# One joining pass for both head groups on eight tiles, T64's last block by VectorE's transposes, and kq products moved ahead, in a two-layer gated DeltaNet and attention encoder

## The chip, the cores and the metric

The kernel runs on one core of a Trainium2 chip. The metric is the device time of one execution in microseconds (us). Before the change it is 744.85, the median of three runs (744.83 to 745.56).

## The reference, cut to what matters

Two layers, 256 tokens of 1024 channels, float32. Each layer normalises its input, multiplies it with one wide input weight, runs two mixers on the parts (a: gated DeltaNet, b: differential attention, 8 heads each), projects both (w_pa, w_pb), merges them with two sigmoid gates and projects again (w_out). The change lies in the DeltaNet mixer. Per head and direction it needs, for each chunk of tokens, the inverse T of a unit lower triangular matrix:

```python
L = jnp.where(strict, jnp.einsum('bhncd,bhnmd->bhncm', kb, k) * decay, 0.0)
T = lax.linalg.triangular_solve(eye + L, jnp.broadcast_to(eye, L.shape),
                                left_side=True, lower=True, unit_diagonal=True)
u = jnp.einsum('bhncm,bhnme->bhnce', T, vb)
w = jnp.einsum('bhncm,bhnmd->bhncd', T, kb * jnp.exp(g)[..., None])
qk = jnp.where(lower, jnp.einsum('bhncd,bhnmd->bhncm', q, k) * decay, 0.0)
```

It runs once forwards and once backwards over the tokens; the two results are added, normalised and gated with silu(z). The attention mixer takes two softmaxes per head, their weighted difference times v, a normalisation per head and a gate with silu(z).

## The kernel before

**Work and order.** TensorE does the projections as chains of 128x512 matmuls in split float32 (a weight and an activation each as a high and a low part, three products: high by high, high by low, low by high; L324 to L326). A projection of 512 columns has 8 k-tiles of 6 matmuls. In the stretch that matters here the projections are, in this order, zb, za (gates of the mixers), gb, ga (the b and the a gate), pb; each has two halves of 512 columns (gb0, gb1, ...). Their 16 k-tiles each give the places 0 to 79: `place(32)` is the first k-tile of gb0, 39 the last, 47 the last of gb1, 48 the first of ga0. All else on TensorE is hung behind such a place (`behind(ins)`), and a scheduler fixes one order for each engine when the kernel is built; every engine works its own queue strictly in that order.

**Weights.** A quarter of a projection's weights (two k-tiles) is loaded by SyncE's queue (`raw_`), cast to the high part by ScalarE (`hi_`, L308) and subtracted to the low part by VectorE (`lo_`, L310). For gb1's second quarter both parts live in `wgb`.

**The triangular inverse.** The kernel treats a chunk of 128 tokens per head, both directions. A forward substitution makes the inverses of the 32-wide diagonal blocks; they go through DRAM into `U_` (transposed blocks, one tile for both groups of four heads) and `T64` (plain blocks, one tile for each group; L898 to L911). Then blocks are joined to 64, then to 128.
- 64-wide joining, in `merges(g)`, once for each group g: y64 = A-block times T64-block, 32 products of 32x32 (L924), copied by ScalarE (L928); zt = y64 transposed times U-block, 32 products (L938), negated by ScalarE into U's off-diagonal blocks (L950); z, the plain form of half of them, 16 products (L943), negated by ScalarE into T64 (L953). Each product works on the 32x32 tile of TensorE's array given by its operands' partitions (rows) and its result's (columns). With `srcdst` these are four tiles, one to a strip of 32 rows, the same four for both groups; z uses two.
- 128-wide joining, in `join()` for both groups at once: y128 = A-block times T64 (64x64, four tiles), copied (L971, L973), then zt with U, negated into U (L981).
- `chunks(g)` then uses U for the recurrence (y1p, sp, ks, y2p, qs, po; L995, L1034).

The steps of `merges` and `join` are placed by a list (L1265): both groups' y64 behind the first kq block (pseudo place 41), zt and z of group 0 at 43, of group 1 at 45, y128 at 48, its zt at 50.

**kq and q's sums.** `weigh_q(g, c)` multiplies k by q for four heads (`gram`, L787, 4 products, called the kq block (g, c) here) and VectorE weighs the result into B (L828). The four of a layer are placed at 39, 42, 44 and 47. `key_sums` (L1042) squares q: VectorE transposes (`tb_q`, L135), ScalarE squares, VectorE sums, then a trip through DRAM on GpSimd's queue and a last sum `ssq` (L1056).

**The attention's end.** The last head's attention (`turn(7)`, `attend(7)`: at and av, L1097 and L1108) stands in gb0 and gb1. ScalarE copies av to `ob` and squares it twice (`sqj`, L1112, L1114), the sums `ssb` go through VectorE (L1239, L1240), GpSimd's power and VectorE (`rb`, L1242); `gate_yb` then gates ob (L1200), transposes it in blocks (`zb`, L249) and sends it through DRAM on GpSimd's queue (L251, L257) to become `ybT` (L263, L265), the input of pb.

PSUM tiles named `bank` and `bank_c` have two buffers each: a third tile waits until the first has been read.

Of the kernel before, what the change touches and what calls it, by code (L numbers as in the profile page):

```python
# [8 lines left out]
F32 = mybir.dt.float32  # L9
# [8 lines left out]
P = 128  # L18
# [3 lines left out]
NM = SEQ // P  # L22
# [27 lines left out]
def hybrid_encoder(  # L50
# [53 lines left out]
    mark = {}  # L104
# [402 lines left out]
    for l in range(DEPTH):  # L507
# [389 lines left out]
        def merges(g):  # L897
# [15 lines left out]
            v4 = lambda ap: ap.rearrange("p (c h i) -> p c h i", c=NM, h=4)  # L913
            y64p = v4(bank_c(f"y64p{l}{g}")[:, :256])
            y64 = work.tile([P, NM, 4, 32], F32, tag="w2c", name=f"y64{l}{g}", bufs=3)

            order = [(c, j4, mm, d) for c, j4 in every for mm in range(2) for d in range(2)]
            order.sort(key=lambda k: k != (0, 0, 1, 1))
            first = mark["pin"]
            for n_, (c, j4, mm, d) in enumerate(order):  # L920
                b0, b1 = srcdst(d, mm)
                co = 32 * (b0 % 2)
                with behind(first):
                    mm_ = T.matmul(y64p[blk(b1), c, j4, :], A[blk(b0), g, c, j4, blk(b1)],  # L924
                                   T64[blk(b0), tix(d, c, j4), co : co + 32], start=True, stop=True)
                if n_ == 0:
                    first = mm_.ins
            S.copy(y64, y64p)  # L928
            yield
            first = mark["pin"]  # L930
            zt64 = v4(bank_c(f"zt64{l}{g}")[:, :256])
            z64 = v4(bank_c(f"z64{l}{g}")[:, :256])
            for c, j4 in every:
                for mm in range(2):
                    for d in range(2):
                        b0, b1 = srcdst(d, mm)
                        with behind(first):
                            T.matmul(zt64[blk(b0), c, j4, :], y64[blk(b1), c, j4, :],  # L938
                                     U[blk(b1), tix(d, c, j4), blk(b1)], start=True, stop=True)
            for c, j4 in every:  # L940
                for d in range(2):
                    b0, b1 = srcdst(d, d)
                    T.matmul(z64[blk(b1), c, j4, :], U[blk(b1), tix(d, c, j4), blk(b1)],  # L943
                             y64[blk(b1), c, j4, :], start=True, stop=True)
            for d in range(2):
                td = slice(8 * d, 8 * d + 8)
                fl = lambda z, b: z[blk(b)].rearrange("p c h i -> p (c h) i")
                for mm in range(2):
                    b0, b1 = srcdst(d, mm)
                    S.mul(U[blk(b0), td, blk(b1)], fl(zt64, b0), -1.0)  # L950
                b0, b1 = srcdst(d, d)
                co = 32 * (b0 % 2)
# [277 lines left out]
        wgb = big.tile([P, 2, 2, 512], F32R, tag="p8", name=f"wgb{l}", bufs=4)  # L1230
        gtb = gate(C_GB, f"gb{l}", "ev",
# [162 lines left out]
```

## Time and profile before

| | before |
|---|---|
| median of three runs | 744.85 us |
| the profiled execution | 744.91 us |
| its span in the profile | 743.0 us |
| TensorE busy | 734.2 us (99%) |
| VectorE busy | 584.4 us (79%) |
| ScalarE busy | 482.2 us (65%) |
| GpSimd busy | 141.0 us (19%) |
| chain that ended last, TensorE's share | 96% |

The span is the time between the first and the last instruction that the profiler saw; the execution's own time holds 1.9 us more around it. A timeline row gives start, length, engine, line, operation, output and inputs by the program's names, shape and number of records merged; in brackets the idle time ahead of it and what ended it. TensorE overlaps matmuls, so the time from one start to the next tells what a matmul costs, not its length. Both layers have the same stretch; in the first it lies from about 219 us to 300 us.

### The profile page before, as it was taken

To read this page: it belongs to the slowest core of one execution; us is meant where nothing else is said; L and a number is where in the kernel's file an instruction comes from. 1 tells how busy PE (TensorE), PEld (TensorE's weight loads), DVE (VectorE), ACT (ScalarE), POOL (GpSimd) and SP (SyncE) were. 2 spreads that over 40 slices of the span, in tenths; PEclk is the share of its full clock that TensorE was granted. 3 is DMA by queue.
4 is the path that set the end of the run, shared out by engine and by line. 5 is a ranking of instruction groups with operands and counts; after the bars stand their busy time and mean duration, and the time that the engine had idled before them with its cause. 6 is when DMAs were issued, how large, how long until landed. Compare 5 with 4: busy or idle time off the path is not lost.

```text
span 743.0 us, 13901 instructions
## 1 busy us (share of the span) xinstructions
PE 734.2 (99%) x5162; PEld 637.3 (86%) x5162; DVE 584.4 (79%) x1111; ACT 482.2 (65%) x1024; POOL 141.0 (19%) x223
## 2 busy tenths in 40 slices
PE   9999999999999999999999999999999999999996
PEld 6999889987888889888889899889788888998885
DVE  8696898999986865578667769899999669538782
ACT  6667875667877586645456578565687758665552
POOL 5004110112022442100000150202110425301000
PEclk9999999999999999999999999999999999999999
DMA  8765667776666462557675466768666747335641
GB/s 262 238 173 170 173 182 198 206 212 196 209 182 175 152 186 89 173 203 244 202 233 141 124 194 192 213 174 230 197 173 197 199 129 224 108 121 204 215 141 57
DMA packets 73733, 135.45 MB, mean 182 GB/s; under 512 B 12912, under 2 KB 13921, under 8 KB 73666
## 3 DMA queue, kind: packets, MB, share of 16 engines
q1 hardware_dynamic: 64750, 113.65, 51.3%
q0 software_dynamic: 7936, 19.35, 8.9%
q10 hardware_dynamic: 980, 1.58, 0.6%
q8 instruction: 40, 0.66, 0.4%
q14 instruction: 27, 0.22, 0.1%
HBM read 125.53 MB, written 9.01 MB: 181 GB/s over the span
## 4 chain that ended last, share of the span: by engine, by line
PE 96%; ACT 2%; issue 1%; DVE 1%; POOLq 0%; POOL 0%; DVEq 0%; ACTq 0%
PE pp_vb L369 4%; PE pp_qk L325 4%; PE pp_qk L326 3%; PE pp_qk L324 3%; PE sc L1070 2%; PE pp_o L369 2%; PE pp_za L325 2%; PE pf_k L385 2%; PE pf_v L385 2%; PE pf_v L389 2%; PE pp_gb L325 2%; PE pp_gb L324 2%; PE pp_zb L324 2%; PE pf_q L387 2%; PE pf_k L389 2%; PE pf_k L387 2%
## 5 line engine op out<-in xcount | busy, mean ns | idle before, releaser
L325 PE MATMUL pp_qk<-lo_qk,hT 128*128 128x512 f32 x128 | 50.5, 394 | 0.3
L326 PE MATMUL pp_qk<-hi_qk,hT 128*128 128x512 f32 x128 | 49.9, 390 | 0.0
L310 DVE TENSOR_TENSOR lo_qk<-raw_qk,hi_qk 128x1024 fp32r<-128x1024 f32 x32 | 39.1, 1221 | 11.1 <-ACT hi_qk L308 10.8
L324 PE MATMUL pp_qk<-hi_qk,hT 128*128 128x512 f32 x128 | 45.1, 393 | 0.0
L308 ACT CAST hi_qk<-raw_qk 128x1024 fp32r<-128x1024 f32 x28 | 29.4, 1050 | 23.4 <-PE pp_qk L326 12.4
L1080 ACT ACTIVATE es<-sc,mx 128x256 f32<-128x256 f32 x64 | 29.7, 474 | 19.6 <-DVE mx L1078 19.6
L310 DVE TENSOR_TENSOR lo_pb<-raw_pb,hi_pb 128x1024 fp32r<-128x1024 f32 x16 | 19.6, 1225 | 24.5 <-ACT hi_pb L308 24.5
L385 PE MATMUL pf_q<-hT,hi_q 128*128 128x256 f32 x128 | 36.1, 285 | 0.0
L387 PE MATMUL pf_q<-hT,hi_q 128*128 128x256 f32 x128 | 35.9, 284 | 0.0
L385 PE MATMUL pf_k<-hT,hi_k 128*128 128x256 f32 x128 | 35.9, 286 | 0.0
L387 PE MATMUL pf_k<-hT,hi_k 128*128 128x256 f32 x128 | 35.9, 285 | 0.0
L385 PE MATMUL pf_v<-hT,hi_v 128*128 128x256 f32 x128 | 35.8, 285 | 0.0
L387 PE MATMUL pf_v<-hT,hi_v 128*128 128x256 f32 x128 | 35.8, 284 | 0.0
L389 PE MATMUL pf_q<-hT,lo_q 128*128 128x256 f32 x128 | 35.2, 288 | 0.0
L389 PE MATMUL pf_v<-hT,lo_v 128*128 128x256 f32 x128 | 34.6, 288 | 0.0
L389 PE MATMUL pf_k<-hT,lo_k 128*128 128x256 f32 x128 | 34.3, 283 | 0.0
L308 ACT CAST hi_pa<-raw_pa 128x1024 fp32r<-128x1024 f32 x16 | 16.9, 1055 | 22.2 <-PE pp_pa L326 16.1
L679 DVE SCALAR_TENSOR_TENSOR cvq<-pf_q,cw,cvq 128x254 f32<-128x254 f32 (+1 forms) x64 | 29.9, 478 | 0.9 <-ACT cvq L675 0.4
L679 DVE SCALAR_TENSOR_TENSOR cvv<-pf_v,cw,cvv 128x254 f32<-128x254 f32 (+1 forms) x64 | 29.8, 476 | 0.1
L325 PEld LDWEIGHTS pp_qk<-lo_qk,hT 128*128 128x128 f32 x128 | 24.0, 188 | 6.7 <-DVE lo_qk L310 1.7
L679 DVE SCALAR_TENSOR_TENSOR cvk<-pf_k,cw,cvk 128x254 f32<-128x254 f32 (+1 forms) x64 | 28.4, 476 | 1.5 <-ACT cvk L675 0.9
L310 DVE TENSOR_TENSOR lo_pa<-raw_pa,hi_pa 128x1024 fp32r<-128x1024 f32 x16 | 19.6, 1224 | 11.2 <-ACT hi_pa L308 11.2
(417 smaller groups left out, 2536.9 us busy)
## 6 DMA issues: line engine op xcount, KB each, us to landing
raw_qk<-in_w_in_dram SPq DMA_DIRECT2D x32, 512.0 KB, 3.8
raw_k<-in_w_in_dram SPq DMA_DIRECT2D x16, 512.0 KB, 4.6
raw_q<-in_w_in_dram SPq DMA_DIRECT2D x16, 512.0 KB, 3.8
raw_v<-in_w_in_dram SPq DMA_DIRECT2D x16, 512.0 KB, 3.8
raw_zb<-in_w_in_dram SPq DMA_DIRECT2D x16, 512.0 KB, 3.9
raw_za<-in_w_in_dram SPq DMA_DIRECT2D x16, 512.0 KB, 3.8
raw_ga<-in_w_in_dram SPq DMA_DIRECT2D x16, 512.0 KB, 4.5
raw_pb<-in_w_pb_dram SPq DMA_DIRECT2D x16, 512.0 KB, 3.8
```

What stands on the lines that cost most here:

```text
L308: high = (V.tensor_copy if kp in turned else S.copy)(hi[:, :, :n], raw[:, :, :n]).ins
L310: mark[nm, kp] = high, V.tensor_tensor(lo[:, :, :n], raw[:, :, :n], hi[:, :, :n].bitcast(F32), ALU.subtract).ins
L324: T.matmul(o, act[kt // 4][:, 0, kt % 4, ts_], hi, start=kt == 0, stop=False)
L325: T.matmul(o, act[kt // 4][:, 0, kt % 4, ts_], lo, start=False, stop=False)
L326: mark["proj"] = T.matmul(o, act[kt // 4][:, 1, kt % 4, ts_], hi, start=False, stop=kt == KT - 1).ins
L369: mark["proj"] = T.matmul(o, act[kt // 4][:, pa, kt % 4, ts_], ws[kt][1 + pw], start=kt == 0 and n_ == 0, stop=kt == KT - 1 and n_ == 2).ins
L385: T.matmul(o, hi[:, cs], act[kt // 4][:, 0, kt % 4, :], start=first, stop=False, skip_group_check=True)
L387: T.matmul(o, hi[:, cs], act[kt // 4][:, 1, kt % 4, :], start=False, stop=False, skip_group_check=True)
L389: T.matmul(o, lo[:, cs], act[kt // 4][:, 0, kt % 4, :], start=False, stop=done, skip_group_check=True)
L679: V.scalar_tensor_tensor(ca[:, o0:o1], acc[:, b, o0 + sft : o1 + sft], cw[:, j, cb : cb + 1], ca[:, o0:o1], ALU.mult, ALU.add)
L1070: mm = T.matmul(sp[n][:, qt * SEQ : (qt + 1) * SEQ], qkT[h // 4][rows, 0, h % 4, qt * P : (qt + 1) * P], qkT[h // 4][rows, 1, h % 4, :], s ...
L1080: S.activation(es[:, n, qt, :], spv[:, qt, :], AF.Exp, bias=mx[:, n, qt : qt + 1], accum_out=s_all[:, h, n, qt : qt + 1])
```

## The change

The 64-wide joining moves from `merges` into `join` and is done for both groups in one pass. Group 1 writes its y64 and zt two blocks of 32 further on (`across`), so that the two groups work on eight tiles of the array, two in each strip of rows. The z products and their PSUM tiles are gone: ScalarE negates zt into U, four pieces first, and VectorE transposes these four in 32x32 blocks from U into T64; then ScalarE negates the other four. ScalarE copies group 1's y64 in two halves. The list of steps becomes y64 behind kq (1,0), zt at 44, y128 at 47 and its zt at 49.

The kq blocks and the last head move: kq (0,0) to place 32, at of head 7 at 34, kq (0,1) to 36, av of head 7 and kq (1,0) to 39, kq (1,1) to 42. q's transposes wait for the a gate's fourth quarter (`ga0`, 3) and not for the last weighing. The second part of `gate_yb` is placed one weight quarter later.

The core of the diff:

```diff
+        def join():
+            across = lambda b, g: (b + 2 * g) % 4
...
+            order = [(c, j4, s2, d, g) for c, j4 in every for g in range(2) for s2 in range(2) for d in range(2)]
...
+                    made = T.matmul(y64p[g][blk(across(b1, g)), c, j4, :], A[blk(b0), g, c, j4, blk(b1)],
+                                    parts[g][1][blk(b0), tix(d, c, j4), co : co + 32], start=True, stop=True)
...
-            S.copy(y64, y64p)
+            S.copy(y64[0], y64p[0])
+            for h_ in range(2):
+                S.copy(y64[1][halves[h_]], y64p[1][halves[1 - h_]])
...
-                    T.matmul(z64[blk(b1), c, j4, :], U[blk(b1), tix(d, c, j4), blk(b1)],
-                             y64[blk(b1), c, j4, :], start=True, stop=True)
...
-                S.mul(T64[blk(b1), td, co : co + 32], fl(z64, b1), -1.0)
...
+                                T.matmul(zt64[g][blk(across(b0, g)), c, j4, :], y64[g][blk(b1), c, j4, :],
+                                         parts[g][0][blk(b1), tix(d, c, j4), blk(b1)], start=True, stop=True)
+            for own in (True, False):
+                for g in range(2):
...
+                        S.mul(U[blk(b0), td, blk(b1)], fl(zt64[g], across(b0, g)), -1.0)
+                        if own:
+                            co = 32 * (b0 % 2)
+                            V.transpose(T64[blk(b1), td, co : co + 32], U[blk(b0), td, blk(b1)])
...
-                with behind(mark["weighed"]):
+                with behind(mark[f"ga{l}0", 3][1]):
                     turn_squares(tb, kq[:, h : h + 2, :, 1, :].rearrange("p h m t -> p (h m) t"))
...
+        def last_head():
+            weigh_q(0, 0, place(32))
+            aT = turn(7, es[7], place(34))
+            weigh_q(0, 1, place(36))
+            attend(7, aT, place(39))
+            weigh_q(1, 0, place(39))
...
-                   (lambda: attend(7, turn(7, es[7], place(34)), place(39)),
-                    lambda: [weigh_q(n // 2, n % 2, place((39, 42, 44, 47)[n])) for n in range(4)]),
+                   (last_head, lambda: weigh_q(1, 1, place(42))),
...
-            at = [mark[f"ga{l}0", m][1] if i else mark[f"gb{l}1", 2 + m][1] for m in range(NM)]
+            at = [mark[f"ga{l}0", 1 + m][1] if i else mark[f"gb{l}1", 2 + m][1] for m in range(NM)]
...
-            mark["pin"] = mark["kq", 0, 0] if at == 41 else place(at)
+            mark["pin"] = mark["kq", 1, 0] if at == 41 else place(at)
...
-        order = [(mg[:2], 41), (mg[:1], 43), (mg[1:2], 45), (mg[2:], 48), (mg[2:], 50)]
+        order = [(mg[2:], 41), (mg[2:], 44), (mg[2:], 47), (mg[2:], 49)]
```

What the scheduler made of it is seen in each engine's row order. VectorE in layer 0, from the split of gb1's last weight quarter (`lo_gb`) to that of ga0's first (`lo_ga`), before; `B` is a weighing of kq, `ob` the gating of y_b, `zb` its transposes:

```order
L310 TENSOR_TENSOR lo_gb_2817<-raw_gb_2818,hi_gb_2816 128x1024
L828 TENSOR_TENSOR B_371<-kq_2834,B_371 128x1024
L1239 TENSOR_TENSOR ssb_382<-ssb_382,r_2860 128x16
L1240 TENSOR_TENSOR ssb_382<-ssb_382,r_2860 128x16
L828 TENSOR_TENSOR B_371<-kq_2840,B_371 128x1024
L1242 SCALAR_TENSOR_TENSOR rb_2862<-rb_2862,r_2860 128x16
L1200 SCALAR_TENSOR_TENSOR ob_0_383<-ob_0_383,rb_2862,zb_0_385 128x128 x8
L249 STREAM_TRANSPOSE zb_0_385<-ob_0_383 128x4x4x32 x2
L828 TENSOR_TENSOR B_371<-kq_2846,B_371 128x1024
L310 TENSOR_TENSOR lo_ga_2896<-raw_ga_2897,hi_ga_2895 128x1024
```

The same stretch after the change, where `T` is T64 (one tile for each group):

```order
L310 TENSOR_TENSOR lo_gb_2835<-raw_gb_2836,hi_gb_2834 128x1024
L1242 TENSOR_TENSOR ssb_382<-ssb_382,r_2860 128x16
L828 TENSOR_TENSOR B_371<-kq_2770,B_371 128x1024
L1243 TENSOR_TENSOR ssb_382<-ssb_382,r_2860 128x16
L828 TENSOR_TENSOR B_371<-kq_2852,B_371 128x1024
L1245 SCALAR_TENSOR_TENSOR rb_2862<-rb_2862,r_2860 128x16
L1197 SCALAR_TENSOR_TENSOR ob_0_383<-ob_0_383,rb_2862,zb_0_385 128x128 x8
L249 STREAM_TRANSPOSE zb_0_385<-ob_0_383 128x4x4x32 x2
L954 STREAM_TRANSPOSE T_2651<-U__96 32x8x32 x2
L954 STREAM_TRANSPOSE T_2658<-U__96 32x8x32 x2
L310 TENSOR_TENSOR lo_ga_2896<-raw_ga_2897,hi_ga_2895 128x1024
```

The third kq weighing (kq_2770, block (1,0)) now stands between the two steps of ssb, the fourth ahead of rb, and the T64 transposes stand behind the gating of y_b and its transposes.

ScalarE from the copy of head 7's av (`ob`) to the copies of y64, before; the cast of gb1's last quarter stands first:

```order
L308 CAST hi_gb_2816<-raw_gb_2818 128x1024
L1112 COPY ob_1_384<-av_2750 128x2x128
L1114 ACTIVATE sqj_312,ssb_382<-ob_1_384 128x128 x2
L928 COPY y_3230<-y64p_3229 128x256
L928 COPY y_3265<-y64p_3264 128x256
L950 ACTIVATE U__96<-zt_3299 32x8x32 x4
L953 ACTIVATE T_2651<-z_3300 32x8x32 x2
```

and after:

```order
L1109 COPY ob_1_384<-av_2762 128x2x128
L1111 ACTIVATE sqj_312,ssb_382<-ob_1_384 128x128
L308 CAST hi_gb_2834<-raw_gb_2836 128x1024
L1111 ACTIVATE sqj_312,ssb_382<-ob_1_384 128x128
L932 COPY y_3231<-y64p_3229 128x256
L934 COPY y_3232<-y64p_3230 64x256 x2
L951 ACTIVATE U__96<-zt_3300 32x8x32 x3
```

The cast now stands between the two squares of ob whose sums VectorE's ssb needs.

On TensorE the wide gb matmuls of a layer (48 of gb0, 48 of gb1) now have between them: av of head 6 with kq (0,0) after 26, at of head 7 after 38, kq (0,1) after 48, av of head 7 after 57, kq (1,0) and all of y64 after 65, kq (1,1) after 66, all of zt after 78, and y128 after 96. Before, av of head 7 with kq (0,0) and y64 stood after 62, and y128 behind ten matmuls of ga0. The 128-wide zt now stands after 21 of ga0, y1p after 36.

More of the change, by code (lines that the diff above doesn't have):

```diff
@@ L912, in merges @@
             yield
+        def join():
             v4 = lambda ap: ap.rearrange("p (c h i) -> p c h i", c=NM, h=4)
[L914 to L918, printed above, removed]
+            fl = lambda z, b: z[blk(b)].rearrange("p c h i -> p (c h) i")
+            across = lambda b, g: (b + 2 * g) % 4
+            y64p = [v4(bank_c(f"y64p{l}{g}")[:, :256]) for g in range(2)]
+            y64 = [work.tile([P, NM, 4, 32], F32, tag="w2c", name=f"y64{l}{g}", bufs=3) for g in range(2)]
+            order = [(c, j4, s2, d, g) for c, j4 in every for g in range(2) for s2 in range(2) for d in range(2)]
+            order.sort(key=lambda k: k[:4] != (0, 0, 1, 1))
@@ L919, in merges @@
             first = mark["pin"]
-            for n_, (c, j4, mm, d) in enumerate(order):
-                b0, b1 = srcdst(d, mm)
+            for n_, (c, j4, s2, d, g) in enumerate(order):
+                b0, b1 = srcdst(d, s2)
                 co = 32 * (b0 % 2)
                 with behind(first):
[L924 to L927, printed above, removed]
@@ L928, in merges @@
-            S.copy(y64, y64p)
+                    made = T.matmul(y64p[g][blk(across(b1, g)), c, j4, :], A[blk(b0), g, c, j4, blk(b1)],
+                                    parts[g][1][blk(b0), tix(d, c, j4), co : co + 32], start=True, stop=True)
+                if n_ < 2:
+                    first = made.ins
+            S.copy(y64[0], y64p[0])
+            for h_ in range(2):
+                S.copy(y64[1][halves[h_]], y64p[1][halves[1 - h_]])
             yield
-            first = mark["pin"]
@@ L931, in merges @@
-            zt64 = v4(bank_c(f"zt64{l}{g}")[:, :256])
-            z64 = v4(bank_c(f"z64{l}{g}")[:, :256])
+            zt64 = [v4(bank_c(f"zt64{l}{g}")[:, :256]) for g in range(2)]
             for c, j4 in every:
-                for mm in range(2):
-                    for d in range(2):
[L936 to L943, printed above, removed]
-                             y64[blk(b1), c, j4, :], start=True, stop=True)
[L945 to L952, printed above, removed]
-                S.mul(T64[blk(b1), td, co : co + 32], fl(z64, b1), -1.0)
+                for g in range(2):
+                    for s2 in range(2):
+                        for d in range(2):
+                            b0, b1 = srcdst(d, s2)
+                            with behind(mark["pin"]):
+                                T.matmul(zt64[g][blk(across(b0, g)), c, j4, :], y64[g][blk(b1), c, j4, :],
+                                         parts[g][0][blk(b1), tix(d, c, j4), blk(b1)], start=True, stop=True)
@@ new lines, in join @@
+            for own in (True, False):
+                for g in range(2):
+                    U, T64 = parts[g]
+                    for d in range(2):
+                        td = slice(8 * d, 8 * d + 8)
+                        b0, b1 = srcdst(d, d if own else 1 - d)
+                        S.mul(U[blk(b0), td, blk(b1)], fl(zt64[g], across(b0, g)), -1.0)
+                        if own:
+                            co = 32 * (b0 % 2)
+                            V.transpose(T64[blk(b1), td, co : co + 32], U[blk(b0), td, blk(b1)])
@@ L954, in merges @@
             yield
-        def join():
-            v4 = lambda ap: ap.rearrange("p (c h i) -> p c h i", c=NM, h=4)
             every4 = [(c, j4, g, d) for c, j4 in every for g in range(2) for d in range(2)]
```

## The prediction

> **What bounds the kernel now.** I read the page first, then who TensorE waited for, then the timeline of TensorE around the joining, and last those of ScalarE and VectorE at the same place.
>
> ```profile
> span 743.0 us, 13901 instructions
> PE 734.2 (99%) x5162; PEld 637.3 (86%) x5162; DVE 584.4 (79%) x1111; ACT 482.2 (65%) x1024; POOL 141.0 (19%) x223
> PE idle L410 <- DVE ones L407: 1.1, 1, 1.1
> PE pp_vb L464 <- ACT wktm_vb L308: 0.3, 1, 0.3
> PE pp_vb L464 <- ACT hT L234: 0.2, 1, 0.2
> PE pp_vb L464 <- DVE wktm_vb L310: 0.2, 1, 0.2
> ```
>
> The first two lines are the page's, the other four the whole answer on TensorE's waits (who waited, for whom, total, times, longest). TensorE is busy 99% of the span, and its four waits lie in the opening. So TensorE's stream sets the end: what it no longer does is gained in full, and any new wait of it is lost in full.
>
> The next rows are TensorE's timeline in layer 0 (start, length, line, tiles, shape, records; a float32 product leaves two records). First the y64 products of both groups with a kq block behind them:
>
> ```profile
> 237.11 0.38 PE L1108 MATMUL av<-vb,aT 128*128 128x128 f32 x2
> ...
> 238.98 1.47 PE L924 MATMUL y64p<-T,A 32*32 32x32 f32 x128
> 240.38 0.50 PE L325 MATMUL pp_gb<-wgb,hT 128*128 128x512 f32 x1
> 240.71 0.39 PE L326 MATMUL pp_gb<-wgb,hT 128*128 128x512 f32 x1
> ...
> 241.41 1.05 PE L787 MATMUL kq<-kq 128*128 128x128 f32 x8
> 242.22 0.47 PE L324 MATMUL pp_gb<-wgb,hT 128*128 128x512 f32 x1
> 242.53 0.39 PE L325 MATMUL pp_gb<-wgb,hT 128*128 128x512 f32 x1
> ...
> 602.16 1.47 PE L924 MATMUL y64p<-T,A 32*32 32x32 f32 x128
> ```
>
> Then the second group's zt and z products, the end of the b gate's projection and the y128 products:
>
> ```profile
> 250.07 0.39 PE L324 MATMUL pp_gb<-hi_gb,hT 128*128 128x512 f32 x1
> 250.39 0.75 PE L938 MATMUL zt<-U__96,y 32*32 32x32 f32 x64
> 251.00 0.69 PE L943 MATMUL z<-y,U__96 32*32 32x32 f32 x32
> 251.62 0.50 PE L325 MATMUL pp_gb<-lo_gb,hT 128*128 128x512 f32 x1
> 251.96 0.40 PE L326 MATMUL pp_gb<-hi_gb,hT 128*128 128x512 f32 x1
> ...
> 253.70 0.48 PE L324 MATMUL pp_ga<-hi_ga,hT 128*128 128x512 f32 x1
> 254.01 0.40 PE L325 MATMUL pp_ga<-lo_ga,hT 128*128 128x512 f32 x1
> ...
> 255.83 0.39 PE L324 MATMUL pp_ga<-hi_ga,hT 128*128 128x512 f32 x1
> 256.15 1.16 PE L964 MATMUL y128p<-T,A 64*64 64x64 f32 x64
> 257.24 0.50 PE L325 MATMUL pp_ga<-lo_ga,hT 128*128 128x512 f32 x1
> ```
>
> What to see: the wide matmuls stand (255.83 - 254.01)/8 = 0.228 us apart. A kq block of 8 records costs 242.53 - 241.41 - 0.23 = 0.89, so 0.11 a record and nothing for its edges. The y64 block holds 1.40 up to the next matmul. A zt and z block costs 251.96 - 250.07 - 2 x 0.228 = 1.43: 0.61 for 64 records of zt on four tiles (9.5 ns each), 0.62 for 32 of z on two tiles (19 ns each), 0.20 for edges. Half the tiles, twice the time a record: the tile is what is slow (38 ns a record), not the issue. The second layer has the same block 363.2 us later, so I work out layer 0 and double it.
>
> **What TensorE itself saves, per layer.** z goes, and the two zt blocks become one, on eight tiles. Now: 2 x 1.43 = 2.87. After: 128 records, 0.20 of edges and about 0.13 of drain (what y64 and z show above pace). If eight tiles halve the pace to 4.75 ns, that is 0.61 + 0.33 = 0.94, a saving of 1.93; if they stay at 9.5, it is 1.55, a saving of 1.32. y64 goes from 1.40 to 0.74, or stays. The four kq blocks, av and at remain as many and only move. So TensorE's own share lies between 1.32 and 2.59.
>
> Which end is likelier hangs on tiles that share a strip of 32 rows, as the eight do in pairs. y128 has four tiles of 64, two to a strip: 16 rounds in 1.09 us, 68 ns a round. Taking turns, 64 columns would cost 34 ns, less than the 38 of zt's 32. So they run at once, and I lean to 2.59. The Trainium skill, page "TensorE: Matmul & The Clock Gate", Part 3, "The mechanism", speaks against it: a weight load overlaps running matmuls only where the row group differs. By that rule the pairs would take turns, and the share would be 1.32; the y128 rows do not bear it out.
>
> **What waits instead.** y128 reads T64, whose last piece came from z by ScalarE. Now VectorE transposes it out of U, and VectorE has it in a fixed order behind the gating of y_b. I follow that queue. ScalarE:
>
> ```profile
> 237.18 1.05 ACT L308 CAST hi_gb<-raw_gb 128x1024 fp32r<-128x1024 f32 x1 [1.50 <-DMA raw_gb<-in_w_in_dram]
> 238.87 0.37 ACT L1112 COPY ob<-av 128x256 f32<-128x256 f32 x1 [0.64 <-PE av L1108]
> 239.27 0.31 ACT L1114 ACTIVATE sqj<-ob 128x128 f32<-128x128 f32 x1
> ...
> 239.71 0.31 ACT L1114 ACTIVATE sqj<-ob 128x128 f32<-128x128 f32 x1
> ...
> 245.27 1.54 ACT L950 ACTIVATE U__96<-zt 32x256 f32<-32x256 f32 x4 [4.17 <-PE zt L938]
> ```
>
> and VectorE, with a group of transposes of a like form last:
>
> ```profile
> 238.25 1.23 DVE L310 TENSOR_TENSOR lo_gb<-raw_gb,hi_gb 128x1024 fp32r<-128x1024 f32 x1 [1.81 <-ACT hi_gb L308]
> 239.40 1.22 DVE L828 TENSOR_TENSOR B<-kq,B 128x1024 f32<-128x1024 f32 x1
> 240.53 0.17 DVE L1239 TENSOR_TENSOR ssb<-ssb,r 128x16 f32<-128x16 f32 x1
> 240.73 0.18 DVE L1240 TENSOR_TENSOR ssb<-ssb,r 128x16 f32<-128x16 f32 x1
> ...
> 244.38 0.18 DVE L1242 SCALAR_TENSOR_TENSOR rb<-rb,r 128x16 f32<-128x16 f32 x1 [0.65 <-POOL rb L156]
> 244.59 2.19 DVE L1200 SCALAR_TENSOR_TENSOR ob<-ob,rb,zb 128x128 f32<-128x128 f32 x8
> 246.69 2.01 DVE L249 STREAM_TRANSPOSE zb<-ob 128x512 f32<-128x512 f32 x2
> 248.55 1.21 DVE L828 TENSOR_TENSOR B<-kq,B 128x1024 f32<-128x1024 f32 x1
> ...
> 278.62 0.26 DVE L1056 TENSOR_REDUCE ssq<-qss 128x16 f32<-128x64 f32 x1 [4.42 <-DMA qss<-qdr]
> ...
> 299.82 0.69 DVE L1036 TENSOR_TENSOR kq<-po,kq 128x512 f32<-128x512 f32 x1 [1.85 <-PE po L1034]
> ```
>
> ```profile
> L135 DVE STREAM_TRANSPOSE tb_q<-kq x8: 656/694/708, 259.0 to 629.8; 128x512 f32<-128x512 f32 x8
> ```
>
> The order of the changed program is: head 7's av, copy, first square, a cast of hi_gb, second square (ScalarE); split of lo_gb, ssb, weighing of kq (1,0), ssb, rb, gating, two transposes, then the four T64 transposes (VectorE). With the steps of these rows, in us of this trace:
> - av of head 7 comes five wide matmuls earlier and behind two kq blocks: 237.11 - 1.14 + 1.78 = 237.75. Its copy started 1.76 after the block's start, when kq's records took turns with av's; six records fewer (0.67) make it 1.09: 238.84.
> - First square +0.40: 239.24. The cast +0.44: 239.68. Its data landed at 237.18 and move by a kq block at most, so they don't hold it.
> - lo_gb starts 1.07 after the cast (238.25 - 237.18): 240.75; ssb +1.15: 241.90; weighing +0.20: 242.10; second ssb +1.13: 243.23. That is 2.50 later than before (240.73).
> - rb +3.65 (the power on GpSimd between): 246.88; gating +0.21: 247.09; transposes +2.10: 249.19; the first T64 transpose +1.86: 251.05.
> - A T64 transpose is 32 x 256 and not in this trace. At half of tb_q's length on top of a fixed part like ssb's: 0.17 + (0.69 - 0.17)/2 = 0.43, and 0.35 apart. Least: plain half, 0.35, 0.27 apart. Most: half of zb's slower pace (1.86/2 = 0.93 apart), 0.63 and 0.55 apart. I take the first, since tb_q too writes whole runs of 32. The fourth is done at 251.05 + 1.05 + 0.43 = 252.53 (least 252.21, most 253.33).
>
> y128's second group cannot start before that. Its first 16 records then have two tiles, the other 32 all four, so the block still needs 1.09: it ends at 252.53 + 0.05 + 1.09 = 253.67. Without the ten a gate matmuls that stood ahead (253.70 to 255.83 and one more, 2.36), it would have ended at 257.24 - 2.36 = 254.88 before. So a layer gains 1.21. TensorE alone would be through at 254.88 - 2.59 = 252.29 to 253.56; it waits 0.1 to 1.4 us, and the pace of eight tiles hardly matters.
>
> **The other edits, at nothing.** ScalarE copies y64 in three pieces and negates zt in eight at 0.385 (1.54/4): 3.1 us. It sat idle 4.17 before that, and 18 wide matmuls, 4.1 us, lie between zt and y128, which needs those banks; gone, that cover would cost what is over 4.1. The first low part of the a gate's weights queues behind the T64 transposes on VectorE, done at about 253.7; TensorE wants it one matmul after y128, at 254.0. If the transposes slip, both slip. q's sums move behind the a gate's fourth part with their store and loads on GpSimd's queue; ssq was there at 278.62, and its first reader follows the products added from 299.82, so some 15 us cover it. On GpSimd the four loads of one y_b tile now go ahead of the next tile's store, on SP one a-gate load goes behind the norm weights: both feed work of later projections. Weighing kq earlier fills VectorE's gaps (1.81 before lo_gb) and is in the steps above.
>
> **Sum.** 2 x 1.21 = 2.4 us. The profiled execution took 744.91 (span 743.0 and 1.9 around it), against a median of 744.85, so the two are one. 744.9 - 2.4 = 742.5. With the least and most of the transposes a layer gains 1.53 or 0.41: 741.8 to 744.1 is this case's own range. A measurement of this kernel can tell 0.2%, 1.5 us, from no change, so 743.4 and 746.4 are the bounds of "same".
>
> **Rivals.**
> - *T64 is ready in time* (0.14). Then all of TensorE's share counts: 2 x 2.59, 739.7; at the four-tile pace 742.3. For it: VectorE has gaps. Against: the queue above is in order, and every step in it has a row.
> - *A small transpose costs what tb_q's costs*, 0.69 and 0.63 apart whatever its size (0.12): done at 251.05 + 1.89 + 0.69 = 253.63, a gain of 0.11 a layer, 744.7: no change.
> - *Slower: it costs what zb's costs*, 1.10 and 0.93 apart, because the piece is cut out of U (0.06): done at 254.94, y128 ends at 256.08, 1.20 lost a layer, 747.3. It decides from 253.74 on, that is four transposes in over 2.69 us. Against it: the piece has half of zb's columns, and its result is written in whole runs of 32.
> - *Slower: eight tiles hinder each other* down to z's 19 ns a record (0.03). y64 then takes 2.6 instead of 1.40, zt 2.8 instead of 2.87, and y128 ends 1.1 later than before: 747.2. The 9.5 ns on four tiles speak against. The same page of the Trainium skill, Part 1, "Wait — 56ns, not 53.3ns?", has starts never closer than 25 ns; by it the change would lose still more, and zt's 9.5 ns contradict it.
>
> The forecast keeps 0.65, of which 0.09 lies above 743.4. Faster: 0.56 + 0.14 = 0.70; same: 0.09 + 0.12 = 0.21; slower: 0.09. The range goes from the middle of the first rival, 740.2, to 744.7; it leaves out the slower cases, half of the first rival and the tail of the second.
>
> **What would show it.** Right: TensorE idle before y128 in both layers, released by VectorE's transpose of T64; rb at about 246.9; T64 transposes near 0.4 us, the first at about 251; y64 and zt blocks under 1 us. Wrong: no wait before y128 (first rival), transposes of 0.7 us or more, y64 above 1.4 us, or a wait elsewhere, first at the a gate's lo part behind y128, whose margin is 0.3.

## The result and the profile after

The changed kernel takes 742.51 us (median of 7 runs, 741.99 to 744.38) against 744.85 (7 runs) before: a ratio of 0.9969, 95% interval 0.9958 to 0.9981. The forecast was 742.5. The profiled execution took 742.73, of which 740.8 is its span, against 744.91 and 743.0.

One line of the page after, and the whole answer on TensorE's waits:

```profile
PE 732.1 (99%) x5034; PEld 635.6 (86%) x5034; DVE 588.5 (79%) x1119; ACT 479.5 (65%) x1018; POOL 140.9 (19%) x223
```

```profile
PE idle L410 <- DVE ones L407: 1.1, 1, 1.1
PE pp_vb L464 <- ACT wktm_vb L308: 0.3, 1, 0.3
PE pp_vb L464 <- ACT hT L234: 0.2, 1, 0.2
```

TensorE has 128 records fewer (z's, in two layers), is busy 2.1 us less, and no wait behind the opening is listed. The predicted wait before y128 is there all the same, but it has to be read from the length of a block. TensorE's timeline in layer 0, each block of the joining with the matmul behind it (start, length, line, tiles, shape, records):

```profile
241.42 1.29 PE L928 MATMUL y64p<-T,A 32*32 32x32 f32 x128
242.64 0.50 PE L326 MATMUL pp_gb<-wgb,hT 128*128 128x512 f32 x1
...
246.70 1.29 PE L943 MATMUL zt<-U__96,y 32*32 32x32 f32 x128
247.92 0.50 PE L324 MATMUL pp_gb<-hi_gb,hT 128*128 128x512 f32 x1
...
252.22 1.79 PE L961 MATMUL y128p<-T,A 64*64 64x64 f32 x64
253.95 0.50 PE L324 MATMUL pp_ga<-hi_ga,hT 128*128 128x512 f32 x1
```

From a block's start to the next matmul, y64 takes 1.22 (1.40 before), zt of both groups 1.22 (the forecast had looked for both under 1 us), and y128 1.73 where it took 1.09. The first group's products issue while the second group's wait, so the row is one and nothing shows as idle.

VectorE's timeline from the second ssb to the first low part of the a gate, with what ended an idle time in brackets:

```profile
242.95 0.17 DVE L1243 TENSOR_TENSOR ssb<-ssb,r 128x16 f32<-128x16 f32 x1
...
246.58 0.17 DVE L1245 SCALAR_TENSOR_TENSOR rb<-rb,r 128x16 f32<-128x16 f32 x1 [1.29 <-POOL rb L156]
246.79 2.19 DVE L1197 SCALAR_TENSOR_TENSOR ob<-ob,rb,zb 128x128 f32<-128x128 f32 x8
248.90 1.99 DVE L249 STREAM_TRANSPOSE zb<-ob 128x512 f32<-128x512 f32 x2
250.92 1.84 DVE L954 STREAM_TRANSPOSE T<-U__96 32x256 f32<-32x256 f32 x4
252.79 1.23 DVE L310 TENSOR_TENSOR lo_ga<-raw_ga,hi_ga 128x1024 fp32r<-128x1024 f32 x1
```

This is the queue that the prediction followed: T64's last transpose ends at 250.92 + 1.84 = 252.76, a little over half a microsecond after y128 began, and y128 ends 1.19 after that (ends of blocks are taken from the start of the matmul behind them).

### The profile page after: what moved, and what is told of

Read it like the earlier page. It is cut to its first block, busy times and chain, and to the rows that moved or that the text cites. A ratio compares the mean times of both kernels' runs of the same rounds, so it can differ in the third digit from the quotient of the medians.

```text
span 740.8 us, 13649 instructions
## 1 busy us (share of the span) xinstructions
PE 732.1 (99%) x5034; PEld 635.6 (86%) x5034; DVE 588.5 (79%) x1119; ACT 479.5 (65%) x1018; POOL 140.9 (19%) x223
## 4 chain that ended last, share of the span: by engine, by line
PE 96%; ACT 2%; issue 1%; DVE 1%; POOLq 0%; POOL 0%; DVEq 0%; ACTq 0%
PE pp_vb L369 4%; PE pp_qk L325 4%; PE pp_qk L326 3%; PE pp_qk L324 3%; PE sc L1067 2%; PE pp_o L369 2%; PE pp_za L325 2%; PE pf_k L385 2%; PE pf_v L385 2%; PE pf_v L389 2%; PE pp_ga L324 2%; PE pp_gb L324 2%; PE pp_zb L324 2%; PE pf_q L387 2%; PE pf_k L389 2%; PE pf_k L387 2%
## 5 line engine op out<-in xcount | busy, mean ns | idle before, releaser
L325 PE MATMUL pp_qk<-lo_qk,hT 128*128 128x512 f32 x128 | 50.5, 394 | 0.3
L325 PEld LDWEIGHTS pp_qk<-lo_qk,hT 128*128 128x128 f32 x128 | 24.0, 188 | 6.6 <-DVE lo_qk L310 1.6
```

The costliest lines, as they stand in the source:

```text
L325: T.matmul(o, act[kt // 4][:, 0, kt % 4, ts_], lo, start=False, stop=False)
```

## The experiments

Theory: TensorE's own work sets the end, the one-run joining saves some of it, and a part of that is lost again because y128 waits for T64 behind VectorE's queue. Rivals: y128 is long for a reason of its own; eight tiles could be faster and something else holds them; the moved kq products or q's sums do the saving.

The opening of single executions differs by up to 1.8 us for reasons that have nothing to do with the edits (see the end). So beside the median I give the stretch from layer 0's first za product to layer 1's first pa product, which holds both joinings and no opening. Its two rows in the profile before, and in that after:

```profile
186.58 0.71 PE L324 MATMUL pp_za<-hi_za,hT 128*128 128x512 f32 x2
...
690.49 0.62 PE L324 MATMUL pp_pa<-hi_pa,yaT 128*128 128x512 f32 x2
```

```profile
186.49 0.71 PE L324 MATMUL pp_za<-hi_za,hT 128*128 128x512 f32 x2
...
688.42 0.61 PE L324 MATMUL pp_pa<-hi_pa,yaT 128*128 128x512 f32 x2
```

That is 503.91 before and 501.93 after, 1.98 less. The granted clock of TensorE is full all through the stretch in every kernel but t64_first and columns. The same two rows of every kernel give (medians are of five to eleven runs; two_strips and columns ran once, 743.13 and 753.92, without a median; the kernel before, run beside the experiments, had 745.0 to 745.1):

| kernel | median us | stretch us | against the changed kernel's stretch |
|---|---|---|---|
| before | 744.85 | 503.91 | +1.98 |
| changed | 742.51 | 501.93 | |
| sums_first | 741.92 | 500.85 | -1.08 |
| sums_rounds | 741.98 | 501.28 | -0.65 |
| sums_y128 | 741.55 | 500.24 | -1.69 |
| rounds_only | 743.53 | 502.47 | +0.54 |
| t64_first | 752.44 | 513.03 | +11.10 |
| t64_twice | 745.59 | 504.75 | +2.82 |
| z_on_tensor | 745.97 | 504.87 | +2.94 |
| kq_back | 745.50 | 503.15 | +1.22 |
| q_sums_back | 743.67 | 502.65 | +0.72 |
| four_tiles | 742.71 | 501.80 | -0.13 |
| two_strips | | 501.94 | 0.0 |
| columns | | 513.18 | +11.25 |

### Does y128 wait for T64?

**t64_twice**: the wait is doubled.

```
+   V.transpose(T64[blk(b1), td, co : co + 32], U[blk(b0), td, blk(b1)])
    V.transpose(T64[blk(b1), td, co : co + 32], U[blk(b0), td, blk(b1)])
```

> Each T64 transpose is made twice, so four more of 0.47 us stand in VectorE's queue in each layer. Theory: y128 ends 1.9 us later in each layer, its block grows from 1.73 to about 3.6, and the time is 742.5 + 3.8 = 746.3. Rival (y128 does not wait for VectorE): at most 0.2 us more in all, 742.5 to 742.7.

Measured: 745.59, the stretch 2.82 longer. The first line of TensorE's waits that is new, and y128 in the timeline:

```profile
PE y128p L962 <- DVE T L955: 2.0, 4, 0.8
```

```profile
253.53 0.76 PE L962 MATMUL y128p<-T,A 64*64 64x64 f32 x20 [0.83 <-DVE T L955]
254.47 1.11 PE L962 MATMUL y128p<-T,A 64*64 64x64 f32 x42 [0.18 <-DVE T L955]
255.51 0.50 PE L324 MATMUL pp_ga<-hi_ga,hT 128*128 128x512 f32 x1
```

Now the wait is long enough to be listed, with VectorE's T64 as its releaser. y128 ends 255.51 - 253.95 = 1.56 later. The last transpose ends at 254.33 in that trace (its last group of three starts at 252.99 and lasts 1.34) against 252.76, 1.57 later: one for one. I had expected 1.9, taking 0.47 for each extra one; here the eight start 0.37 to 0.47 apart. The rival's 0.2 is out.

**sums_first**: the wait is removed further up the queue.

```
             attend(7, aT, place(39))
+            mark["last_sq"] = mark["sq"]
+            V.reciprocal(r0, s_all[:, :, 0, :].rearrange("p h q -> p q h"))
+            V.tensor_tensor(ssb, ssb, r0, ALU.mult)
+            mark["ssb"] = V.tensor_tensor(ssb, ssb, r0, ALU.mult).ins
             weigh_q(1, 0, place(39))
...
-   later={1: (0, None)} if i and places[i][1] is not None else None,
+   later={1: (0, None), **late()} if i and places[i][1] is not None else None,
...
+   ({2: rgb[:, 0], 3: rgb[:, 1]}, {}), late=lambda: {3: (mark["last_sq"], mark["ssb"])})
```

> ScalarE squares both halves of head 7 before the last cast of hi_gb, and VectorE forms ssb twice before it splits the last lo_gb; weighing kq (1,1) falls behind the gating. Theory (the queue behind head 7's sums decides): the second ssb moves from 242.95 to about 240.1, rb from 246.58 to about 243.8, y_b's transposes to about 247.2, and the T64 transposes then follow ScalarE's negations, the last done at about 251.1, before y128 could start at 252.2. The y128 block goes from 1.73 to 1.09 us: 742.5 - 1.3 = 741.2. Rival (the wait is elsewhere): 742.5. If the later lo_gb or kq (1,1) is wanted sooner than I think, TensorE waits in the second b gate projection, and the time is over 742.5.

Measured: 741.92; the stretch is 1.08 shorter. VectorE, and y128 on TensorE:

```profile
240.16 0.17 DVE L1237 TENSOR_TENSOR ssb<-ssb,r 128x16 f32<-128x16 f32 x1
...
243.80 0.17 DVE L1246 SCALAR_TENSOR_TENSOR rb<-rb,r 128x16 f32<-128x16 f32 x1 [0.53 <-POOL rb L156]
...
249.30 1.84 DVE L954 STREAM_TRANSPOSE T<-U__96 32x256 f32<-32x256 f32 x4
```

```profile
252.10 1.48 PE L961 MATMUL y128p<-T,A 64*64 64x64 f32 x64
253.50 0.50 PE L324 MATMUL pp_ga<-hi_ga,hT 128*128 128x512 f32 x1
```

ssb, rb and T64 come when expected: T64 is done at 251.14, about 1 us before y128 starts. But y128 still takes 1.40, not 1.09. So the wait costs 1.73 - 1.40 = 0.33 a layer; the other 0.31 is no wait. It is y128's order: in the changed program eight products of the first group stand first, then eight of the second, and only then do the two groups alternate. 32 of the 64 records so run on two tiles at about 29 ns (the 58 ns of a four-tile round, two at a time) in place of 14.5: 32 x 14.5 = 0.46 is the most that order can cost. At y128 the two layers gain 0.33 and 0.37 of the 1.08; the other 0.35 comes behind y1p in layer 0, and has to do with q's sums (see the sum, below).

**sums_rounds, rounds_only, sums_y128**: the order of y128's products.

```
+   made = mark["pin"]
    for c, j4, g, d in every4:
-       with behind(mark["pin"]):
-           T.matmul(ps[g][halves[1 - row(d) if g == 0 else row(d)], c, j4, :],
+       with behind(made):
+           made = T.matmul(ps[g][halves[1 - row(d) if g == 0 else row(d)], c, j4, :],
```

> As sums_first, and y128's products are issued in rounds over all four tiles from the start, where the scheduler had put 16 records of the first group and 16 of the second ahead. Theory (what was left of y128's 1.40 us in sums_first is those 32 records on two tiles at 29 ns in place of four at 14.5): the block goes to 1.09 us, and the kernel from 741.9 to 741.3. Rival (1.40 us is what y128 takes when nothing holds it in this program): 741.9.

> y128's products in rounds over four tiles, head 7's sums as in the changed kernel. Theory (the last T64 transpose is done at 252.76, and nearly all of y128 stands behind it in either order): y128 ends at about 252.8 + 1.1 = 253.9 as now, 742.5. Rival (the two-tile stretch is a loss of its own): 0.3 us a layer less, 741.9.

In sums_rounds y128 takes 1.10 as expected, yet the time does not fall (741.98). The same edit also applies to the 64x64 zt products of the 128-wide joining behind, and there the scheduler now slips two a-gate matmuls in between:

```profile
258.19 0.33 PE L962 MATMUL zt<-U__96,y 64*64 64x64 f32 x4
...
259.12 1.15 PE L962 MATMUL zt<-U__96,y 64*64 64x64 f32 x60
```

From y128's start to y1p's it takes 11.15 us, against 11.03 in sums_first: the 0.30 won are given back with 0.12 more, some 0.42 for cutting the block in two. rounds_only has the same cut without the earlier sums: 743.53, and neither theory nor rival had that in it. Its y128 ends at 254.46, 1.69 after its start at 252.77, against 1.73 in the changed kernel, so the order by itself gains next to nothing while the wait is there, as the theory has it. With that order the wait shows in TensorE's list, once in each layer, though T64's transposes stand where the changed kernel has them:

```profile
PE y128p L962 <- DVE T L954: 0.3, 2, 0.2
```

sums_y128 chains y128 alone:

> As sums_first, and only y128's products, not the 64-wide zt's behind them, are issued in rounds over four tiles; on every engine nothing else differs from sums_first. Theory (in sums_rounds y128 fell to 1.10 us, but the same edit cut the 64-wide zt products in two around two a-gate matmuls, which took it back): y128 takes 1.10, zt stays in one piece at 1.10, the start of y128 to that of y1p falls from 11.03 to 10.72, and the time from 741.9 to 741.3. Rival (the start of y1p is set by something else, such as the negations on ScalarE): 11.03 and 741.9 stay.

```profile
253.90 1.16 PE L962 MATMUL y128p<-T,A 64*64 64x64 f32 x64
254.99 0.50 PE L324 MATMUL pp_ga<-hi_ga,hT 128*128 128x512 f32 x1
```

y128 takes 1.09, y128 to y1p 10.74, the stretch 688.43 - 188.19 = 500.24. The median is 741.55 (741.14 to 742.76), ratio to the kernel before 0.9950, interval 0.9937 to 0.9964. That is the fastest kernel here; its median is 0.96 below the changed kernel's, though the two intervals still touch.

**t64_first**: the transposes of T64 ahead of y_b's.

```
+   run(jn, 41)
+   run(jn, 44)
    gate_yb(0)
...
-   sent[i, m] = tb, send(tb, ov, f"{nm}{i}{m}")
+   sent[i, m] = tb, send(tb, ov, f"{nm}{i}{m}", None if i else mark["t64"])
...
+   with behind(after):
        V.transpose(tb.rearrange("p j (d k) -> p j k d", k=4), src.rearrange("p k (j t) -> p j k t", j=4))
```

> VectorE transposes the four pieces of T64 ahead of y_b's two transposes instead of behind them; nothing else moves on TensorE, ScalarE or SyncE. Theory (VectorE's queue sets when y128 may start, 0.64 us a layer are lost inside the y128 block): T64 is done by about 250.8, y128 starts without a wait, its block shrinks from 1.73 to about 1.09 us, and the kernel takes 742.5 - 1.3 = 741.2. Rival 1 (the longer y128 block is its own pace or waits for something else): the block stays at 1.7, 742.5. Rival 2 (y_b's transposes, now 1.8 us later with their store and loads, are wanted in time): the block shrinks, but a wait comes up around the first use of ybT, 742.5 or more.

Measured: 752.44. Rival 2 is right, and more costly than thought. One line of TensorE's waits, and one of ScalarE's timeline:

```profile
PE y1p L993 <- ACT U__96 L979: 7.1, 2, 3.8
```

```profile
263.99 1.20 ACT L264 ACTIVATE ybT<-zb,nw 128x512 fp32r<-128x512 f32 x1 [6.42 <-DMA zb<-bny_yb]
```

y128 shrank to 1.41 as in sums_first. But y_b's transposes end 1.66 later (252.55 against 250.89), ScalarE's ybT copy waits 6.42 us for the data that go out to memory and back, and it stands in ScalarE's queue ahead of the negations that y1p needs. In the changed kernel that copy started at 259.67, here at 263.99: 1.66 us at the transposes have become 3.35 where the loads start (256.33 against 252.98 on GpSimd) and 4.32 at the copy; why the trip grew is not shown. An engine that waited 1.59 us there already had no room for more. The 7.1 us of waits, one in each layer, are not all of the loss: behind each the granted clock of TensorE is 0.50, for 3.4 us in layer 0 and 6.8 in layer 1. Half of TensorE's busy time there, some 4 us, is my estimate of what that cost.

### Are eight tiles slow, and why?

**four_tiles** (leaves out the right data of the second group's y64, whose copies still take the halves as if the tiles were spread):

```
-   across = lambda b, g: (b + 2 * g) % 4
+   across = lambda b, g: b
```

> Both groups' y64 and zt products use the same four tiles instead of eight, in the same order. Theory (a strip of 32 rows takes one product at a time, whatever tile it goes to): y64 and zt keep their 1.22 us, 742.5. Rival 1 (eight tiles run at once, and something else, such as issue, holds them at 8.3 ns a record): four tiles fall back to the 9.5 to 11 ns that before's rows show, 0.15 to 0.3 us more in each block, of which the y64 part counts: 742.5 to 743. In either case less than the 1.27 us a layer by which my forecast leaned to eight tiles.

**two_strips**:

```
-   A[blk(b0), g, c, j4, blk(b1)], parts[g][1][blk(b0), tix(d, c, j4), co : co + 32]
+   A[blk(b0 % 2), g, c, j4, blk(b1)], parts[g][1][blk(b0 % 2), tix(d, c, j4), co : co + 32]
...
-   for g in range(2):
-       for s2 in range(2):
-           for d in range(2):
+   for s2 in range(2):
+       for d in range(2):
+           for g in range(2):
```

> Leaves the right data out of y64: its products read blocks 0 and 1 in place of blocks 2 and 3 as well, so that 128 records use two strips of 32 rows and all eight places of the result. zt's products keep their data and tiles, but the two products that share a strip of rows follow one another. Theory (one product at a time in a strip of rows, 33 ns each): y64 takes 128 x 16.6 ns, a block of about 2.2 us; zt keeps 1.22 to 1.4. Rival (about 8.3 ns a record is the rate of issue, and the strips do not matter): y64 stays at 1.22.

**columns**:

```
+   for e in (0, 16):
...
-   parts[g][1][blk(b0), tix(d, c, j4), co : co + 32]
+   parts[g][1][blk(b0), tix(d, c, j4), co + e : co + e + 16]
...
-   parts[g][0][blk(b1), tix(d, c, j4), blk(b1)]
+   parts[g][0][blk(b1), tix(d, c, j4), halves[b1 // 2]]
```

> y64's products are cut into two of 16 columns, 256 records in place of 128; zt's products read 64 columns in place of 32, of which 32 are used. Theory a (a strip is held some 33 ns by a record, whatever its columns): y64 doubles to about 2.3 us, zt stays at about 1.2. Theory b (it is held by the column): y64 stays at about 1.2 us, zt doubles to about 2.3. y128's 58 ns for four tiles in two strips of 64 rows, that is 29 ns a record of 64 columns, speaks for a.

y64 in four_tiles, then in two_strips:

```profile
241.86 1.33 PE L928 MATMUL y64p<-T,A 32*32 32x32 f32 x128
243.13 0.50 PE L326 MATMUL pp_gb<-wgb,hT 128*128 128x512 f32 x1
```

```profile
241.82 1.35 PE L928 MATMUL y64p<-T,A 32*32 32x32 f32 x128
243.10 0.50 PE L326 MATMUL pp_gb<-wgb,hT 128*128 128x512 f32 x1
```

With four tiles in place of eight y64 takes 1.27 instead of 1.22, zt 1.22 as before, and the whole is 742.71: the spread over eight tiles is worth 0.05 us a layer in y64 and nothing that can be seen in the time (y128, which waits for T64, is 0.04 shorter). So far both theories stood. two_strips decides: all 128 records of y64 on two strips of 32 rows (four tiles, two to a strip) take 1.28, not 2.2, and putting the two products of a strip behind one another leaves zt at 1.21. My theory that a strip takes one product at a time falls. What is left is a rate of about 1.22/128 = 9.5 ns a record with edges, the same for four tiles, eight tiles and two strips; only before's z, on two tiles, was at 19. In columns, y64 and then zt:

```profile
241.38 1.67 PE L929 MATMUL y64p<-T,A 32*32 32x16 f32 x159
245.43 1.11 PE L929 MATMUL y64p<-T,A 32*32 32x16 f32 x97 [2.39 <-issue]
...
252.13 1.47 PE L944 MATMUL zt<-U__96,y 32*32 32x64 f32 x128
253.53 0.50 PE L324 MATMUL pp_gb<-hi_gb,hT 128*128 128x512 f32 x1
```

Half the columns do not make a record shorter (1.67/159 = 10.5 ns), and twice the columns make zt 1.40 instead of 1.22. A record costs nearly the same whatever its width: theory a for the width, though not for its reason. Issue is the likeliest holder of that rate; no run shows it by itself. The 256 records in one run bring a stop marked as issue, 2.39 us in layer 0 and 2.36 in layer 1, 4.8 of the 11.25 us that this kernel lost. Behind the stops the granted clock is 0.50, as in t64_first for 3.4 and 6.8 us, and two wide matmuls start 0.43 apart in place of 0.23; by the same estimate that is some 4 us more.

### What are the moves worth?

**z_on_tensor**:

```
+   T.matmul(z64[g][blk(across(b0, g)), c, j4, :], parts[g][0][blk(b1), tix(d, c, j4), blk(b1)],
+            y64[g][blk(b1), c, j4, :], start=True, stop=True)
...
-   V.transpose(T64[blk(b1), td, co : co + 32], U[blk(b0), td, blk(b1)])
+   V.tensor_scalar(T64[blk(b1), td, co : co + 32], fl(z64[g], across(b0, g)), -1.0, None, ALU.mult)
```

> z is formed on TensorE again, 64 more records behind zt in each layer, on the same four tiles a group as zt; VectorE scales it into T64 in place of the transposes, at the same place of its queue. Theory (VectorE's queue, not TensorE's own sum, sets when y128 ends): zt and z together take about 0.6 us more in each layer, but y128 would have waited that long: 742.5, within 0.4 either way with the unknown length of the scaling from PSUM (0.2 to 0.5 a piece). Rival (what TensorE does is what counts, as everywhere else in this kernel): 742.5 + 1.2 = 743.7.

Measured: 745.97, the stretch 2.94 longer, more than the rival had. It does not tell the two apart, for the edit brought a wait of its own. ScalarE's negations, which shared a bank with z:

```profile
253.07 0.83 ACT L960 ACTIVATE U__96<-zt 32x256 f32<-32x256 f32 x2 [1.79 <-DVE T L963]
```

They stop 1.79 us for VectorE's scaling, the a gate's first cast slips behind, and y128 starts 7.43 after zt instead of 5.52. It shows only that z on TensorE costs 2.00 - 1.22 = 0.78 us of TensorE's time a layer (in layer 1 with a stop of 0.44 on top, marked as issue), and that a piece scaled by VectorE out of PSUM takes as long as a transposed one: 421 ns in the mean against 437.

**kq_back**:

```
-   weigh_q(0, 0, place(32))
    aT = turn(7, es[7], place(34))
-   weigh_q(0, 1, place(36))
    attend(7, aT, place(39))
-   weigh_q(1, 0, place(39))
...
-   lambda: weigh_q(1, 1, place(42))
+   lambda: [weigh_q(n // 2, n % 2, place((39, 42, 44, 47)[n])) for n in range(4)]
...
-   mark["pin"] = mark["kq", 1, 0] if at == 41 else place(at)
+   mark["pin"] = mark["kq", 0, 0] if at == 41 else place(at)
```

> The four kq products go back behind head 7's av, to the places that they had before the change; the one-run joining and the transposes stay. TensorE does the same work in another order. Theory (the moved kq blocks gain nothing on TensorE and only push head 7's sums, and with them T64, back): rb comes at about 244.4 as before the change, T64 is done at about 251.6 with one weighing of kq ahead of it, y128 does not wait, and the time is 741.3 to 741.9. Rival (kq ahead of head 7 is what saves time, by av and kq taking turns or by the weighing): 743 or more.

Measured: 745.50, the stretch 1.22 longer. My theory was wrong: in the changed kernel the move does save time on TensorE. TensorE around zt in layer 0, beginning and end, and y128 in layer 1:

```profile
246.55 0.38 PE L787 MATMUL kq<-kq 128*128 128x128 f32 x2
246.86 0.24 PE L943 MATMUL zt<-U__96,y 32*32 32x32 f32 x2
...
248.64 1.24 PE L943 MATMUL zt<-U__96,y 32*32 32x32 f32 x122
249.80 0.50 PE L324 MATMUL pp_gb<-hi_gb,hT 128*128 128x512 f32 x1
...
617.99 1.16 PE L961 MATMUL y128p<-T,A 64*64 64x64 f32 x64
```

At the same place the scheduler interleaves kq's products with zt's. From 246.55 to 249.80 are 3.25 us for what takes 0.89 + 1.22 + 0.09 = 2.20 apart (0.09 is what zt in the changed kernel starts late behind a wide matmul): 1.05 for changing between 128-wide and 32-wide tiles a few products at a time, and the same in layer 1. y128 is cut the same way in layer 0 (254.02 to 256.54, 2.52 for 0.89 + 1.09 + 0.09, 0.45 lost), but runs in one piece in layer 1. Against that stand 0.64 a layer won where T64 is no longer waited for and y128 runs in rounds. In layer 1 a low part of the a gate also comes late, which costs 0.25. Up to y1p that makes 1.05 + 0.45 - 0.64 = 0.86 in layer 0 and 1.05 - 0.64 + 0.25 = 0.66 in layer 1; the traces show 0.84 and 0.65. Behind y1p layer 0 gets 0.35 back, the same 0.35 as in sums_first.

**q_sums_back**:

```
-   with behind(mark[f"ga{l}0", 3][1]):
+   with behind(mark["weighed"]):
        turn_squares(tb, kq[:, h : h + 2, :, 1, :].rearrange("p h m t -> p (h m) t"))
```

> q's block transposes, squares and sums may start as soon as they could before the change, not behind the a gate's fourth part. On VectorE the first transpose of q then comes between y_b's gating and its last transpose, behind the T64 transposes; sp's products move behind two a-gate matmuls. Theory (VectorE has room in the a gate's projection, T64 is ahead of all this): 742.5, within 0.3. Rival (the a gate's lo parts or y_b's transposes come late behind q's): 743 to 745, with TensorE waiting for them.

Measured: 743.67, the stretch 0.72 longer, the rival's sign. VectorE, and TensorE around the matmul (L325) that reads the low part formed there:

```profile
258.80 0.70 DVE L135 STREAM_TRANSPOSE tb_q<-kq 128x512 f32<-128x512 f32 x1
...
260.37 1.20 DVE L310 TENSOR_TENSOR lo_ga<-raw_ga,hi_ga 128x1024 fp32r<-128x1024 f32 x1
```

```profile
261.13 0.39 PE L324 MATMUL pp_ga<-hi_ga,hT 128*128 128x512 f32 x1
261.62 0.50 PE L325 MATMUL pp_ga<-lo_ga,hT 128*128 128x512 f32 x1
```

One transpose of q ahead of lo_ga makes it end at 261.57, and its matmul starts 0.49 after the one before instead of 0.23: 0.26 in layer 0, in layer 1 0.30, together 0.56 of the 0.72, again too short to be listed as a wait.

## Why the prediction was right, step by step

**The queue: right.** All steps of ScalarE and VectorE came within 0.3 us of their forecast: the second ssb at 242.95 (243.23), rb at 246.58 (246.88), the first T64 transpose at 250.92 (251.05). A T64 transpose takes 437 ns (0.43 forecast), but four in a row are (1.84 - 0.44)/3 = 0.47 apart, not 0.35, so the last was done at 252.76 instead of 252.53, and y128 ended at 253.95 instead of 253.67.

**TensorE's share: mis-sized.** "I lean to 2.59" failed, and with it "the tile is what is slow". Measured are 1.40 - 1.22 = 0.18 for y64 and 1.36 + 1.43 - 1.42 = 1.37 for zt and z, together 1.55 a layer, near the low end (1.42 is 248.26 - 246.38 - 2 x 0.228 with zt's neighbours; 1.36 is the first group's block before, 245.97 - 244.15 - 2 x 0.228, which the prediction took to be 1.43 like the second's). The reason given for leaning was that tiles sharing a strip run at once. That inference holds up (two_strips), but there was next to nothing to win by it: four tiles already had the rate (four_tiles). Of y64's 0.18 the spread explains 0.05; the rest came with the merging of the groups and the order of the products, which no run takes apart. By the rule of the Trainium skill, page "TensorE: Matmul & The Clock Gate", Part 3, "The mechanism", the share was to be 1.32, near the measured one; but two_strips contradicts it as the reason: 128 records on two row groups, two tiles in each, took 1.28 us.

**The wait before y128: right in kind, smaller than forecast.** With the share of 2.59 the wait would have been 1.4 us a layer; with the measured 1.55 the forecast's own rows give 253.67 - (254.88 - 1.55) = 0.34. y128 lost 1.73 - 1.09 = 0.64. Taking T64 away first gains 0.33 of it (sums_first), the order that puts 32 records on two tiles then 0.31 (sums_y128); the order alone gains 0.04, since the wait then takes its place (rounds_only). The prediction saw that order and counted it only behind the wait. It also wanted TensorE idle in the rows; a wait inside a block of two independent groups shows as length.

**The sum: the right number, in part by luck.** The forecast gain of 1.21 a layer was for the end of y128. There (start of the a gate's 13th wide matmul, against the layer's first za product) the changed kernel is ahead by 0.91 in layer 0 and 0.97 in layer 1, about 1.55 - 0.64. The missing 0.3 is mostly T64's, whose end came 0.23 later than forecast in a layer that began 0.09 earlier. Two things that the prediction did not count bring it near 1.21 again. The first is a gain: the 128-wide zt takes 262.02 - 260.64 = 1.38 up to the next matmul before and 260.05 - 258.95 = 1.10 after, 0.28 less (0.27 in layer 1).

```profile
260.64 1.44 PE L964 MATMUL zt<-U__96,y 64*64 64x64 f32 x64
```

```profile
258.95 1.17 PE L961 MATMUL zt<-U__96,y 64*64 64x64 f32 x64
```

Before, its first records start in pairs 58 ns apart, as y128's in sums_first do; after, four of them start in 58 ns all through. That fits an order on two tiles and one on four, but no run changes this order alone.

The second is a loss in layer 0. VectorE and TensorE in the changed kernel:

```profile
284.20 0.27 DVE L1053 TENSOR_REDUCE ssq<-qss 128x16 f32<-128x64 f32 x1 [2.53 <-DMA qss<-qdr]
284.38 2.15 DVE L1012 SCALAR_TENSOR_TENSOR vtm<-ks,nE,vtm 128x128 f32<-128x128 f32 x8
285.55 1.16 PE L992 MATMUL y2p<-vtm,U__96 128*128 128x128 f32 x8
```

q's sums, which the change moved, make VectorE wait 2.53 us for data from memory. The prediction saw 15 us of cover for the reader of ssq, but vtm stands behind ssq in VectorE's queue, and TensorE's y2p needs vtm. From the first qs product (284.81) to the next wide matmul (287.72) it is 2.91 in layer 0 against 2.60 in layer 1; in sums_first, where ssq comes at 283.35, it is 2.60 in layer 0 too. That is nearly all of the 0.35 behind y1p.

So layer 1 gains 1.55 - 0.64 + 0.28 = 1.19 and layer 0 0.31 less, 0.88. From za to pa the traces have 1.21 and 0.83, and 0.06 is lost between the layers: 1.98. The rest up to the 2.18 between the two profiled executions lies in the opening and the tail, and the medians differ by 2.34. The price of being later in VectorE's queue and that of slower tiles hardly add, as the prediction said: in four_tiles y64 is 0.05 longer in each layer and y128 0.04 to 0.05 shorter. No larger case was run.

**The edits at nothing: two were not nothing.** Undoing q's sums alone costs 0.72 in the stretch, undoing the kq move alone 1.22. What they would do in the kernel before was not run. In the changed kernel they keep the run of small tiles in one piece and q's transposes from crowding out the a gate's low parts; q's sums cost 0.31 in layer 0 besides, as shown above. ScalarE's eight negations were covered, as forecast (last one done at 251.14, y128 at 252.22).

## What to carry to other kernels

Read the length of a block as well as the idle column: two groups that issue in one row hide the wait of the second, and a start-to-start spacing one matmul wide hides a wait of a quarter microsecond. Small-tile products belong in one run: each cut by a 128-wide matmul cost about 0.2 us at each edge here, more than the spread over more tiles could bring. When a step moves onto an in-order queue, move the slow producer ahead of it (head 7's sums) rather than the step ahead of the others; t64_first shows the price of the second way. And when a step that waits for memory moves on such a queue, ask what stands behind it, not only who reads it.

## What the runs showed of the hardware

- From four 32 x 32 tiles on, float32 records go at 9.5 to 10 ns each with edges, whether on four tiles, eight, or two strips of rows; two tiles took 19. 16, 32 or 64 columns changed a record by about 15% (10.5, 9.5 and 10.9 ns).
- 256 such records in one run stopped for 2.39 and 2.36 us (columns), 192 for 0.44 in one layer of two (z_on_tensor), marked as issue; 128 did not stop.
- Behind stops of TensorE of 2.4 to 3.8 us (columns, t64_first) the granted clock fell to 0.50, for 3.4 us in layer 0 and 6.8 in layer 1 of both runs. In no other run did it fall in the stretch.
- The length of the opening varies. In the profile of z_on_tensor, kq_back and sums_y128 the eight transposes of the first tile (pt_h) took 1.91 to 1.92 us, against 1.04 to 1.32 in the others, and everything behind was up to 1.8 us late. The Trainium skill, page "TensorE: Matmul & The Clock Gate", Part 1, "The HAM clock gate", has the clock rise at a moment that varies from run to run, as a window runs free of the kernel's start; half speed for the same products fits, and the trace's first entry of a full granted clock is at 10.6 to 10.7 us in these three and at 4.4 to 6.9 in the others. That is a wider variation than the 0.5 us that the Trainium skill gives there.
